# First MLP product computed token-major, with a seven-product two-by-two scheme for half of its K pairs

## Chip, core and metric

One core of a Trainium2 chip runs the whole program. The metric is the device time of one execution in microseconds (us); below, "stage" means a stretch of that execution. In the profile PE is TensorE's matrix multiplication, PEld its weight load (the loading of the stationary operand), DVE is VectorE, ACT is ScalarE, POOL is GpSimd, SP is SyncE (here it only issues DMAs).

## What is computed

One layer on 256 tokens of width 2048: a token mixer (two groups of recurrent heads, between an input and an output projection), then a squared-ReLU MLP with 8192 hidden units, each around a residual. The change concerns the first product of the MLP.

```python
h = h + hybrid_token_mixer(rms_norm(h, norm_mix_w), ...)
n = rms_norm(h, norm_ffn_w)
h = h + jnp.square(jax.nn.relu(n @ w_ff1)) @ w_ff2     # (256, 2048) @ (2048, 8192), then @ (8192, 2048)
out = rms_norm(h, norm_final_w)
```

All data are float32. The row factor of the second norm is positive and is taken out of the product: the kernel multiplies by the weight column `norm_ffn_w` before the first product and by the squared row factor `fs` after the second one.

## The kernel before, in words

**Products in three parts.** A float32 operand is split into a rounded part `hi` (type fp32r, what TensorE reads) and a remainder `lo`. A product is then hi·hi + hi·lo + lo·hi, all added up in one PSUM bank. `split` (L111) makes the parts of a weight tile: ACT casts to `hi` (L117), then DVE subtracts, `lo = w - hi` (L118). Both read SBUF; the subtraction has two SBUF inputs.

**Weights.** The weight matrices stream through three buffers `w` of 1 MB (L85, L99), filled by DMAs of SP's queue in program order. A buffer is filled again when its last `split` is done. `hi`/`lo` have three buffers of 1024 columns each (`spool`, L86).

**Stages.** (1) The input projection and the mixer, L166 to L627. (2) The output projection, L643 to L670, in two halves `nh` of 1024 output columns: 16 K steps with 12 products of 512 columns each into four banks; at the end of a half DVE adds the banks to the residual `h` (L660), ACT squares for the norm (L662), PE transposes the half's eight 128-column blocks to feature-major (L669) and `to_T` (L161) evicts each to `hT` as hi (ACT, L162) and lo (DVE, L163). (3) The first MLP product, L689 to L706, below. (4) The second, L721 to L742: for each of 64 hidden blocks, 24 products with a token-major stationary operand `gs` and 512 moving weight columns, into eight banks; the last three blocks are held back and interleaved with the final norm and the stores.

**The first MLP product** works feature-major: the weights stand still, the tokens move. Sixteen groups `fg` of four hidden blocks; a group reads four weight tiles; each K block and hidden block costs one matmul with `hi` stationary and 512 moving columns (the 256 tokens' hi and lo side by side, L700) and one with `lo` stationary and 256 moving columns (L701). At the end of a group ACT and DVE evict: copy, add, and `max(x,0)*x` into `g` (L703 to L706). So the hidden activations come out with the hidden unit on the partition, as the second product wants its stationary operand. POOL has no work in stages 3 and 4 except two tiny powers at the end.

**Order.** The Tile framework schedules the instructions of each engine from the data dependences and its own estimates, so the order of an engine's queue is not the text's; each engine runs its queue in order. PSUM has eight banks: four in `psA` and four in `psB`.

The residual `h` stays in SBUF from the output projection to the end of the program.

Of the kernel before, what the change touches and what calls it, by code (L numbers as in the profile page):

```python
# [73 lines left out]
def hybrid_block(ctx: ExitStack, tc: tile.TileContext, x, xt, w_in, w_ab, params, w_out, w_ff1, w_ff2,  # L74
# [555 lines left out]
    psB = ctx.enter_context(tc.tile_pool(name="psB", bufs=4, space=PSUM))  # L630
# [4 lines left out]
    hT = bpool.tile([P, KT, 2 * T], F32R, tag="xT", name="hT")
    h = bpool.tile([P, 2 * D], F32, tag="h", name="h").rearrange("p (f c) -> p f c", f=2)
    for hf in range(2):
        SP.dma_start(h[:, hf, :], x[hf * P:(hf + 1) * P, :])
    octx = ExitStack()
    op = octx.enter_context(tc.tile_pool(name="op", bufs=1))  # L640
    sqj = op.tile([P, 1024], F32, tag="sqj", name="sqj")
    fs = cpool.tile([P, 16], F32, tag="fs", name="fs")
    for nh in range(2):  # L643
        accs = [acc_a() for _ in range(4)]
        for kp in range(8):
            w = wtile()
            SP.dma_start(w, w_out[nh * 8 + kp])
            for kk in range(2):
                k = 2 * kp + kk
                hi, lo = split(w[:, kk * 1024:(kk + 1) * 1024], 1024)  # L650
                for hf in range(2):
                    for a, ww in ((0, hi), (T, hi), (0, lo)):
                        st = yT(k, a + hf * P, a + hf * P + P)
                        for c in range(2):
                            PE.matmul(accs[2 * hf + c], lhsT=st, rhs=ww[:, c * 512:(c + 1) * 512],  # L655
                                      start=(k == 0 and a == 0 and ww is hi), stop=(k == 2 * NH - 1 and ww is lo))
        for hf in range(2):
            for c in range(2):
                hv = h[:, hf, nh * 1024 + c * 512:nh * 1024 + (c + 1) * 512]
                DVE.tensor_tensor(out=hv, in0=accs[2 * hf + c], in1=hv, op=ALU.add)  # L660
            hv = h[:, hf, nh * 1024:(nh + 1) * 1024]
            ACT.activation(sqj, hv, AF.Square, accum_out=fs[:, 2 * hf + nh:2 * hf + nh + 1])  # L662
        for k2 in range(4):
            pt = acc_b()
            for kk in range(2):
                k = nh * 8 + k2 * 2 + kk
                ptk = pt[:, kk * T:(kk + 1) * T]
                for hf in range(2):
                    PE.transpose(ptk[:, hf * P:(hf + 1) * P], h[:, hf, k * P:(k + 1) * P], ident)  # L669
                to_T(hT, k, ptk, cols[:, 16 + k:17 + k])  # L670
# [7 lines left out]


    fp = ctx.enter_context(tc.tile_pool(name="fp", bufs=1))  # L680
    NF = DFF // P
    NG = NF // 2
    gt = [fp.tile([P, NG, T], F32, tag=f"g{i}", name=f"g{i}") for i in range(2)]

    def g(f):
        return gt[f // NG][:, f % NG, :]

    nfw = fp.tile([P, D], F32, tag="nfw", name="nfw")
    for fg in range(NF // 4):  # L689
        accs = [acc_a() if fg % 2 == 0 else acc_b() for _ in range(4)]  # L690
        for kq in range(4):
            w = wtile()
            SP.dma_start(w, w_ff1[fg * 4 + kq])
            for q in range(2):
                hi, lo = split(w[:, q * 1024:(q + 1) * 1024], 1024)
                for kk in range(2):
                    k = 4 * kq + 2 * q + kk
                    for f in range(4):
                        cs = slice(kk * 512 + f * P, kk * 512 + (f + 1) * P)
                        PE.matmul(accs[f], lhsT=hi[:, cs], rhs=hT[:, k, :], start=(k == 0), stop=False)  # L700
                        PE.matmul(accs[f][:, T:], lhsT=lo[:, cs], rhs=hT[:, k, 0:T], start=False, stop=(k == KT - 1))  # L701
        for f in range(4):
# [6 lines left out]
    accs = [[acc_a() for _ in range(4)], [acc_b() for _ in range(4)]]  # L709
    TAIL = 3  # L710
    held = []

# [5 lines left out]
                      start=(f == 0 and a == 0 and ww is hi), stop=(f == NF - 1 and ww is lo))  # L718

    keep = None  # L720
    for f in range(NF):  # L721
        w = wtile()
        SP.dma_start(w, w_ff2[f])
        gs = fp.tile([P, 2 * T], F32R, tag="gs", name="gs", bufs=4)
        split(g(f), None, gs[:, 0:T], gs[:, T:])
# [4 lines left out]
        for q in range(2):  # L730
            qs = slice(q * 1024, (q + 1) * 1024)
            if 0 <= n < TAIL - 1:
                hl.append(split(w[:, qs], None, keep[:, n, 0, qs], keep[:, n, 1, qs]))
            else:
                hl.append(split(w[:, qs], 1024))
        if n >= 0:
            held.append((f, gs, hl))
            continue
        for q in range(2):
            for hf in range(2):  # L740
                for c in (2 * q, 2 * q + 1):
                    ff2(f, hf, c, gs, hl)  # L742
    fin = fp.tile([P, 12], F32, tag="fin", name="fin")
    sqf = fp.tile([P, 512], F32, tag="sqf", name="sqf")
    o = fp.tile([P, D], F32, tag="o", name="o", bufs=1)
# [30 lines left out]
def _laid_out(i):  # L776
# [5 lines left out]
    for base in (0, 4112):  # L782
        v = w[:, base:base + 4096].reshape(2, 8, P, 2, 2, NH, P)
        groups.append(v.transpose(5, 3, 0, 2, 1, 4, 6).reshape(4 * NH, P, 2048))

    def columns(a):
        return a.reshape(-1, P).T

# [34 lines left out]
```

## Time and profile before

| | |
|---|---|
| median of 3 runs (lowest, highest) | 1283.92 us (1283.6, 1284.52) |
| the profiled execution | 1285.84 us |
| its span, first to last instruction | 1283.9 us |
| mean granted TensorE clock | 0.992 of full speed |
| stage 1, to the first output projection product | 455 us |
| stage 2 | 455 to 563.8 us |
| stage 3, the first MLP product | 563.8 to 926.8 us |
| stage 4, the second, and the end | 926.8 to 1283.9 us |

All durations below come from the profiled execution; its span is within 0.1 us of the runs' median, so a difference worked out on the span is applied to the median. Matmuls are pipelined: a 512-column matmul is shown with some 0.39 us, but the next one starts after a little over half of that, so what counts is the distance of starts. Times in brackets in a timeline row are idle time of the engine ahead of the instruction and what ended it.

### The profile page before, as it was taken

The page shows a single profiled execution, that of the slowest core. Times are in us where ns is not written, and L with a number is a line of the kernel's source. Part 1 is how long each engine was busy: PE and PEld are TensorE (multiplying, and loading weights), DVE is VectorE, ACT ScalarE, POOL GpSimd, SP SyncE. Part 2 cuts the span into 40 slices and gives each one's busy share as a digit, 9 for nine tenths or more (in the row PEclk, how much of TensorE's full clock was granted, in tenths as well). Part 3 has the DMA queues.
Part 4 walks back from the last instruction along what each step waited for, and adds up shares of the span by engine and source line. Part 5 has one row for each costly group of instructions (what it writes and reads, how often), then busy time and mean ns, then how long its engine had stood idle before and what let it go on. Part 6 is the DMA issues. An engine that isn't in the chain of part 4 may idle for free.

```text
span 1283.9 us, 18498 instructions
## 1 busy us (share of the span) xinstructions
PE 1252.5 (98%) x7290; PEld 1063.2 (83%) x7290; DVE 858.5 (67%) x1200; ACT 673.8 (52%) x972; POOL 180.4 (14%) x224
## 2 busy tenths in 40 slices
PE   6999999998899999999999999999999999999997
PEld 5888888877788887888888888888888888888885
DVE  8789999888867996565556555565555555555556
ACT  7567677655556874454444443444444444444453
POOL 4233433278301121000000000000000000000000
PEclk9999999998999999999999999999999999999999
DMA  7455555543423644455555555555555555555552
GB/s 289 166 160 184 174 180 192 171 140 131 149 100 131 217 151 168 154 203 191 194 173 190 196 174 189 197 175 186 197 195 190 188 191 192 194 194 197 197 200 95
DMA packets 34646, 229.65 MB, mean 179 GB/s; under 512 B 4408, under 2 KB 5184, under 8 KB 7808
## 3 DMA queue, kind: packets, MB, share of 16 engines
q1 hardware_dynamic: 32256, 225.32, 49.8%
q0 software_dynamic: 1728, 2.11, 1.3%
q8 instruction: 57, 0.93, 0.3%
q10 hardware_dynamic: 576, 1.05, 0.2%
q14 instruction: 29, 0.24, 0.1%
HBM read 225.83 MB, written 2.63 MB: 178 GB/s over the span
## 4 chain that ended last, share of the span: by engine, by line
PE 91%; DVE 3%; POOL 3%; issue 2%; DMA 1%; ACT 0%; SPq 0%; POOLq 0%; DVEq 0%; ACTq 0%
PE acc L281 15%; PE acc L717 14%; PE accb L717 13%; PE accb L700 9%; PE acc L700 9%; PE acc L282 8%; PE acc L655 7%; PE accb L701 5%; PE acc L701 5%; POOL Xt L419 1%; POOL X L421 1%; PE pd L575 1%; DVE xT L163 1%; DMA big<-in_xt_dram 1%; PE pk L363 1%
## 5 line engine op out<-in xcount | busy, mean ns | idle before, releaser
L118 DVE TENSOR_TENSOR lo<-w,hi 128x1024 fp32r<-128x1024 f32 x408 | 511.5, 1255 | 364.6 <-ACT hi L117 364.1
L117 ACT CAST hi<-w 128x1024 fp32r<-128x1024 f32 (+1 forms) x416 | 432.6, 1042 | 447.3 <-PE accb L717 177.2
L281 PE MATMUL acc<-xT,hi 128*128 128x512 f32 x1024 | 363.2, 401 | 9.6 <-ACT hi L117 8.5
L282 PE MATMUL acc<-xT,lo 128*128 128x256 f32 x1024 | 282.8, 285 | 4.8 <-DVE lo L118 4.7
L281 PEld LDWEIGHTS acc<-xT,hi 128*128 128x128 f32 x1024 | 191.0, 190 | 49.1 <-ACT hi L117 8.5
L282 PEld LDWEIGHTS acc<-xT,lo 128*128 128x128 f32 x1024 | 194.8, 191 | 12.1 <-DVE lo L118 6.2
L700 PE MATMUL acc<-hT,hi 128*128 128x512 f32 x512 | 181.3, 399 | 0.0
L700 PE MATMUL accb<-hT,hi 128*128 128x512 f32 x512 | 180.8, 398 | 0.0
L717 PE MATMUL accb<-hi,gs 128*128 128x512 f32 x496 | 170.6, 389 | 0.0
L701 PE MATMUL accb<-hT,lo 128*128 128x256 f32 x512 | 143.2, 281 | 0.0
L701 PE MATMUL acc<-hT,lo 128*128 128x256 f32 x512 | 142.8, 281 | 0.0
L717 PE MATMUL acc<-hi,gs 128*128 128x512 f32 x496 | 133.4, 389 | 0.0
L700 PEld LDWEIGHTS accb<-hT,hi 128*128 128x128 f32 x512 | 96.1, 188 | 23.9
L700 PEld LDWEIGHTS acc<-hT,hi 128*128 128x128 f32 x512 | 96.1, 188 | 23.4
L159 POOL TENSOR_TENSOR fin<-fin,cst 128x1 f32<-128x1 f32 x2 | 1.1, 566 | 777.0 <-PE accb L717 769.5
L717 PEld LDWEIGHTS acc<-hi,gs 128*128 128x128 f32 x496 | 93.0, 188 | 19.4
L717 PEld LDWEIGHTS accb<-hi,gs 128*128 128x128 f32 x496 | 93.1, 188 | 19.3
L701 PEld LDWEIGHTS acc<-hT,lo 128*128 128x128 f32 x512 | 96.5, 189 | 0.2
L701 PEld LDWEIGHTS accb<-hT,lo 128*128 128x128 f32 x512 | 96.6, 189 | 0.1
L717 PE MATMUL accb<-lo,gs 128*128 128x512 f32 x248 | 95.8, 389 | 0.0
L717 PE MATMUL acc<-lo,gs 128*128 128x512 f32 x248 | 77.2, 389 | 0.0
L717 PEld LDWEIGHTS acc<-lo,gs 128*128 128x128 f32 x248 | 46.6, 188 | 9.7
(248 smaller groups left out, 1323.6 us busy)
## 6 DMA issues: line engine op xcount, KB each, us to landing
w<-in_w_ff_dram SPq DMA_DIRECT2D x128, 1024.0 KB, 4.9
w<-in_w_in_dram SPq DMA_DIRECT2D x62, 1024.0 KB, 5.0
w<-in_w_out_dram SPq DMA_DIRECT2D x16, 1024.0 KB, 4.9
big<-in_xt_dram SPq DMA_DIRECT2D x4, 512.0 KB, 7.9
w<-in_w_in_dram SPq DMA_DIRECT2D x4, 512.0 KB, 8.1
h<-in_x_dram SPq DMA_DIRECT2D x2, 1024.0 KB, 9.2
dt<-scr_g POOLq DMA_DIRECT2D x8, 128.0 KB, 5.6
nfw<-in_norm_final_w_dram SPq DMA_DIRECT2D x1, 1024.0 KB, 4.7
```

Source lines behind the costliest of these rows:

```text
L117: ACT.copy(hi, w)
L118: eng.tensor_tensor(out=lo, in0=w, in1=hi.bitcast(F32), op=ALU.subtract)
L163: DVE.scalar_tensor_tensor(out=dst[:, k, T:2 * T], in0=pt, scalar=wcol, in1=dst[:, k, 0:T].bitcast(F32), op0=ALU.mult, op1=ALU.subtract)
L281: PE.matmul(accs[g], lhsT=hi[:, kk, g, :], rhs=xT[:, k, :], start=(k == 0), stop=False)
L282: PE.matmul(accs[g][:, T:], lhsT=lo[:, kk, g, :], rhs=xT[:, k, 0:T], start=False, stop=(k == KT - 1))
L363: PE.matmul(pk0, lhsT=R[:, 1, 0:P], rhs=qk.rearrange("p a t -> p (a t)"), start=True, stop=True)
L419: POOL.tensor_tensor(out=t3, in0=X[:, j, j + 1:].unsqueeze(2).to_broadcast([np_, nr, ncol]), in1=X[:, j, 0:ncol].unsqueeze(1).to_broadcast ...
L421: POOL.tensor_tensor(out=X[:, j + 1:, 0:ncol], in0=X[:, j + 1:, 0:ncol], in1=t3, op=ALU.subtract)
L655: PE.matmul(accs[2 * hf + c], lhsT=st, rhs=ww[:, c * 512:(c + 1) * 512], start=(k == 0 and a == 0 and ww is hi), stop=(k == 2 * NH - 1 and ...
L700: PE.matmul(accs[f], lhsT=hi[:, cs], rhs=hT[:, k, :], start=(k == 0), stop=False)
L701: PE.matmul(accs[f][:, T:], lhsT=lo[:, cs], rhs=hT[:, k, 0:T], start=False, stop=(k == KT - 1))
L717: PE.matmul(accs[hf][c], lhsT=gs[:, a + hf * P:a + hf * P + P], rhs=ww[:, cs], start=(f == 0 and a == 0 and ww is hi), stop=(f == NF - 1 a ...
```

## The change

The first MLP product is turned round. The tokens (128 at a time) become the stationary operand and 512 weight columns move; the result is token-major, so PE has to transpose it afterwards. The 2048-long contraction is taken in eight pairs `kp` of two 128-blocks, one weight tile each, and the hidden units in eight groups `ng` of 1024, that is two blocks of 512. For a pair, the activations are a 2×2 block matrix (two token halves × two K blocks) and the weights another (two K blocks × two hidden blocks).

- Four pairs (2, 4, 6, 7) are multiplied plainly: 8 block products of three matmuls, 24 matmuls of 512 columns.
- Four pairs (`SUMS`: 0, 1, 3, 5) use a Winograd-Strassen scheme with seven block products, 21 matmuls. It needs sums of the activation blocks (made once, at the end of the output projection, and kept as `sets`) and four sums of the weight blocks for each tile. The weight sums T1, T2, T4 and one in place are made by POOL, each a 128x512 tensor_tensor with two SBUF inputs; they and the original blocks are split as before, 3.5 times 1024 columns for a tile instead of 2.
- Each of the seven products has a bank of its own; after the last of the four pairs DVE combines p1, p5, p6, p7 in `C4`, and after the last pair it adds p2, p3, p4, p8. ACT applies relu. The transposes (16 for a group, in four bundles, with ACT's square as eviction) are put between products of the next group as `fills`, through bank 8.
- `h` no longer stays in SBUF: each half goes to DRAM (`scr_h`) as soon as it is summed, and comes back, with the last norm's weights, after the last product that reads `sets`, by loads on SP's queue.
- The hi/lo pairs have two more buffers (five); the constants come in two DMAs, the larger part in a buffer that is given up after stage 1. All eight PSUM banks are one pool in stages 3 and 4.

```diff
+            X = op.tile([P, 8, P], F32, tag="X", name="X", bufs=2)
+            ACT.activation(view(X, P, [[-P, 2], [1, P]]), pt[:, 0:T].rearrange("p (a t) -> p a t", a=2), AF.Copy, scale=wc[0])
+            ACT.activation(X[:, 2:4, :].rearrange("p a t -> p (a t)"), pt[:, T:2 * T], AF.Copy, scale=wc[1])
+            DVE.tensor_tensor(out=X[:, 4], in0=X[:, 0], in1=X[:, 3], op=ALU.add)
...
+            split(X[:, 1:8], None, st[:, 0], st[:, 1])
...
+        pool, t = (spool, "") if n % 5 < 3 else (fp, "2")
+        return [pool.tile([P, 1024], F32R, tag=p + t, name=p + t, bufs=2 if t else 3) for p in ("hi", "lo")]
...
+    def product(dst, a, b, start, stop):
+        (ah, al), (bh, bl) = a, b
+        PE.matmul(dst, lhsT=ah, rhs=bh, start=start, stop=False)
+        PE.matmul(dst, lhsT=al, rhs=bh, start=False, stop=False)
+        PE.matmul(dst, lhsT=ah, rhs=bl, start=False, stop=stop)
...
+            for c in range(4):
+                PE.transpose(pt[:, c * P:(c + 1) * P], src[:, c * P:(c + 1) * P], ident)
+            ACT.activation(g(8 * ng + 4 * half, 4)[:, :, hf * P:(hf + 1) * P], pt.rearrange("p (c t) -> p c t", c=4),
+                           AF.Square)
...
-                        PE.matmul(accs[f], lhsT=hi[:, cs], rhs=hT[:, k, :], start=(k == 0), stop=False)
-                        PE.matmul(accs[f][:, T:], lhsT=lo[:, cs], rhs=hT[:, k, 0:T], start=False, stop=(k == KT - 1))
-        for f in range(4):
-            lot = fp.tile([P, T], F32, tag="lotf", name="lotf", bufs=2)
-            ACT.copy(lot, accs[f][:, T:])
-            DVE.tensor_tensor(out=lot, in0=accs[f][:, 0:T], in1=lot, op=ALU.add)
-            DVE.scalar_tensor_tensor(out=g(4 * fg + f), in0=lot, scalar=0.0, in1=lot, op0=ALU.max, op1=ALU.mult)
+            SP.dma_start(w, w_ff1[ng * KP + kp])
...
+                POOL.tensor_tensor(out=T1, in0=b12, in1=w[:, 512:1024], op=ALU.subtract)
+                POOL.tensor_tensor(out=T2, in0=b22, in1=T1, op=ALU.subtract)
+                POOL.tensor_tensor(out=T4, in0=b21, in1=T2, op=ALU.subtract)
+                POOL.tensor_tensor(out=b12, in0=b22, in1=b12, op=ALU.subtract)
+                B21, B22 = halves(split_pair(w[:, 1024:2048]))
+                B1, B2 = halves(split_pair(TT[:, 0:1024]))
+                B4 = [tp.tile([P, 512], F32R, tag=t, name=t) for t in ("hi4", "lo4")]
+                split(T4, None, *B4)
+                B3, B11 = halves(split_pair(w[:, 0:1024]))
...
+                for dst, a, b in ((p2, 1, B21), (p3, 6, B22), (p5, 3, B1), (p6, 4, B2), (p4, 2, B4), (p7, 5, B3),
+                                  (p1, 0, B11)):
+                    product(dst, A[a], b, kp == 0, kp == LAST_SUMS and a in (0, 3, 4, 5))
...
+                for kk, b1, b2 in ((0, B11, B12), (1, B21, B22)):
+                    for dst, hf, b in ((p2, 0, b1), (p3, 0, b2), (p4, 1, b1), (p8, 1, b2)):
+                        product(dst, A(kk, hf), b, first and kk == 0 and dst is p8, last and kk == 1)
+        for n, (at, p) in enumerate(((0, p2), (2, p3), (1, p4), (3, p8))):
+            DVE.tensor_tensor(out=C4[:, at], in0=p, in1=C4[:, at], op=ALU.add)
+        for n in range(4):
+            ACT.activation(C4[:, n], C4[:, n], AF.Relu)
+            fills.append(turn(ng, n, C4[:, n]))
+    for hf in range(2):
+        SP.dma_start(h[:, hf, :], scr_h[hf])
```

The order of instructions moves most at three places.

PE at the seam between stages 2 and 3. Before (L655: output projection; L669: transposes of the second half; L700, L701: first MLP product):

```order
L655 MATMUL acc<-hi,yTb 128x512 x4
L655 MATMUL acc<-lo,yTb 128x512 x2
L669 MATMUL accb<-cst,h 128x128 x2
L700 MATMUL acc<-hT,hi 128x512
L701 MATMUL acc<-hT,lo 128x256
```

Now (L675, L690 and L756 to L758 in their places):

```order
L675 MATMUL acc<-hi,yTb 128x512 x4
L675 MATMUL acc<-lo,yTb 128x512 x2
L690 MATMUL accb<-cst,h 128x128 x16
L756 MATMUL p_5701<-hi,sets 128x512
L757 MATMUL p_5701<-hi,sets 128x512
L758 MATMUL p_5701<-lo,sets 128x512
```

The sixteen transposes stood in eight pairs between products of the next stage; now they stand in one row, and the first MLP product is behind all of them.

DVE in the middle of the first MLP product. Before, one group (L705, L706: the eviction):

```order
L118 TENSOR_TENSOR lo<-w,hi 128x1024 x7
L705 TENSOR_TENSOR lotf<-accb,lotf 128x256 x2
L706 SCALAR_TENSOR_TENSOR g_5652<-lotf 128x256 x2
L118 TENSOR_TENSOR lo<-w,hi 128x1024
```

Now, from the end of one group to the third tile of the next (L120 is `split`'s subtraction; `TT` holds the weight sums T1, T2, T4; `C` is C4, `p` a bank):

```order
L829 TENSOR_TENSOR C_7026<-p_6751,C_7026 128x512
L829 TENSOR_TENSOR C_7026<-p_6752,C_7026 128x512
L120 TENSOR_TENSOR lo_7135<-w,hi_7134 128x1024
L829 TENSOR_TENSOR C_7026<-p_6753,C_7026 128x512
L120 TENSOR_TENSOR lo_7179<-w,hi_7178 128x1024
L829 TENSOR_TENSOR C_7026<-p_6879,C_7026 128x512
L120 TENSOR_TENSOR lo_7131<-TT,hi_7130 128x512
L120 TENSOR_TENSOR lo<-TT,hi 128x1024
L120 TENSOR_TENSOR lo_7234<-w,hi_7233 128x1024
L120 TENSOR_TENSOR lo<-w,hi 128x1024 x2
L120 TENSOR_TENSOR lo_7187<-TT,hi_7186 128x512
L120 TENSOR_TENSOR lo_7270<-w,hi_7269 128x1024
```

The splits of a group are no longer alone: the bank additions stand among them, and splits of `TT`, which POOL must have written.

POOL before: the last rows of stage 1 (L550, L599), then the two powers of the final norm (L159):

```order
L538 TENSOR_TENSOR u<-u 128x256
L541 TENSOR_SCALAR gx<-gx 128x256
L550 TENSOR_TENSOR E<-gx 128x256
L599 TENSOR_TENSOR A<-rd,cst 128x128 x2
L159 TENSOR_TENSOR fin<-fin,cst 128x1 x2
```

Now, after stage 1 (L703: activation sums of the output projection; L788 to L791: the weight sums of tile 0; L791 is the one in place):

```order
L603 TENSOR_TENSOR A<-rd,cst_a 128x128 x2
L703 TENSOR_TENSOR X<-X 128x128 x3
L788 TENSOR_TENSOR TT<-w 128x512
L789 TENSOR_TENSOR TT<-w,TT 128x512
L791 TENSOR_TENSOR w<-w 128x512
L790 TENSOR_TENSOR TT<-w,TT 128x512
```

The last four stand there thirty-two times, sixteen rows for each of the eight groups, where POOL had nothing.

More of the change, by code (lines that the diff above doesn't have):

```diff
@@ L627, in hybrid_block, with a_plain, a_sums @@
     mctx.close()
[L630 removed]
+    octx = ExitStack()
+    psB = octx.enter_context(tc.tile_pool(name="psB", bufs=4, space=PSUM))
     def acc_b():
         return psB.tile([P, 512], F32, tag="accb", name="accb")
[L635 to L636 removed]
+    SUMS = (0, 1, 3, 5)
+    sets = bpool.tile([P, 8192], F32R, tag="xT", name="sets")
+    sets2 = ctx.enter_context(tc.tile_pool(name="ap", bufs=1, side="right")).tile([P, 3584], F32R, tag="s2", name="sets2")
+    plain = [kp for kp in range(KT // 2) if kp not in SUMS]
+    def a_plain(kp):
+        n = plain.index(kp)
+        return sets[:, n * 1024:(n + 1) * 1024].rearrange("p (k s) -> p k s", k=2)
+    def a_sums(kp):
+        n = SUMS.index(kp)
+        t, at = (sets, 4096 + n * 1792) if n < 2 else (sets2, (n - 2) * 1792)
+        return t[:, at:at + 1792].rearrange("p (s n t) -> p s n t", s=2, n=7)
+    h = hpool.tile([P, 2 * D], F32, tag="h", name="h").rearrange("p (f c) -> p f c", f=2)
+    scr_h = dpool.tile([2, P, D], F32, tag="scr_h", name="scr_h")
     for hf in range(2):
         SP.dma_start(h[:, hf, :], x[hf * P:(hf + 1) * P, :])
[L639 removed]
     op = octx.enter_context(tc.tile_pool(name="op", bufs=1))
@@ new lines, in g, with bank, pair, split_pair @@
+    def g(f, n=1):
+        return gt[f // NG][:, f % NG:f % NG + n, :]
+    def bank(i):
+        return psF.tile([P, 512], F32, tag=f"p{i}", name=f"p{i}")
+    pairs = [0]
+    def pair():
+        n = pairs[0] = pairs[0] + 1
+        pool, t = (spool, "") if n % 5 < 3 else (fp, "2")
+        return [pool.tile([P, 1024], F32R, tag=p + t, name=p + t, bufs=2 if t else 3) for p in ("hi", "lo")]
+    def split_pair(w):
+        hi, lo = pair()
+        split(w, None, hi, lo)
+        return hi, lo
@@ new lines, in halves, with turn, go @@
+    def halves(hl):
+        return [[t[:, c * 512:(c + 1) * 512] for t in hl] for c in range(2)]
+    def turn(ng, n, src):
+        half, hf = n // 2, n % 2
+        def go():
+            pt = bank(8)
+            for c in range(4):
+                PE.transpose(pt[:, c * P:(c + 1) * P], src[:, c * P:(c + 1) * P], ident)
+            ACT.activation(g(8 * ng + 4 * half, 4)[:, :, hf * P:(hf + 1) * P], pt.rearrange("p (c t) -> p c t", c=4),
+                           AF.Square)
+        return go
@@ L707, in hybrid_block @@
+    t1.close()
+    f2 = ctx.enter_context(tc.tile_pool(name="f2", bufs=1, side="right"))
+    tail = bpool.tile([P, 8192], F32, tag="xT", name="tail")
+    h, nfw, o = tail[:, 0:2 * D].rearrange("p (f c) -> p f c", f=2), tail[:, 2 * D:3 * D], tail[:, 3 * D:]
+    for hf in range(2):
+        SP.dma_start(h[:, hf, :], scr_h[hf])
     SP.dma_start(nfw, norm_final_w.unsqueeze(0).to_broadcast([P, D]))
-    accs = [[acc_a() for _ in range(4)], [acc_b() for _ in range(4)]]
+    accs = [[None] * 4, [None] * 4]
@@ L710, in hybrid_block @@
+    for hf, c, i in ((0, 0, 1), (0, 1, 5), (1, 0, 6), (1, 1, 7), (0, 2, 2), (0, 3, 3), (1, 2, 4)):
+        accs[hf][c] = bank(i)
     TAIL = 3
@@ L720, in hybrid_block @@
     keep = None
+    late = []
     for f in range(NF):
@@ L734, in hybrid_block @@
             else:
-                hl.append(split(w[:, qs], 1024))
+                hl.append(split_pair(w[:, qs]))
         if n >= 0:
@@ L741, in hybrid_block @@
                 for c in (2 * q, 2 * q + 1):
[L742 to L745, printed above, removed]
+                    if f < 2 and (hf, c) == (1, 3):
+                        late.append((f, hf, c, gs, hl))
+                    else:
+                        ff2(f, hf, c, gs, hl)
+                    fill()
+        if f == 1:
+            accs[1][3] = bank(8)
+            for a in late:
+                ff2(*a)
+            c1.close()
+    fin = f2.tile([P, 12], F32, tag="fin", name="fin")
+    sqf = f2.tile([P, 512], F32, tag="sqf", name="sqf")
     NP = 5
```

91 lines of the change are left out of this document (69 added, 22 removed).

## The prediction

> **What bounds the kernel now.** I read the page first: busy times, and the share of the chain that ended last.
>
> ```profile
> span 1283.9 us, 18498 instructions
> PE 1252.5 (98%) x7290; PEld 1063.2 (83%) x7290; DVE 858.5 (67%) x1200; ACT 673.8 (52%) x972; POOL 180.4 (14%) x224
> PE 91%; DVE 3%; POOL 3%; issue 2%; DMA 1%; ACT 0%; SPq 0%; POOLq 0%; DVEq 0%; ACTq 0%
> ```
>
> PE ends the program. Busy matmuls overlap, so the stages tell more: the windows of stage 3 and of stage 4's products, then the same windows for L118 (DVE's remainder subtraction) alone.
>
> ```profile
> core 0: us, PE busy (x) PEld busy (x) DVE busy (x) ACT busy (x) POOL busy (x), PEclk, DMA share, GB/s
> 563.80:926.80 363.00, 363.00 (x2065) 315.00 (x2064) 205.22 (x270) 160.30 (x206) 0.00 (x0) 1.00 0.54 189
> 926.80:1274.90 348.10, 348.10 (x1538) 288.07 (x1536) 187.67 (x212) 156.85 (x203) 0.58 (x1) 1.00 0.54 188
> 563.80:926.80 363.00, 158.24 (x132) 0.00 (x0) 1.00 0.54 189
> ```
>
> In stage 3 PE never idles at a full clock (1.00), DVE works 205 of 363 us, POOL nothing. The waits say who is late:
>
> ```profile
> ACT hi L117 <- PE accb L700: 95.2, 64, 1.8
> ACT hi L117 <- PE acc L700: 92.0, 62, 1.8
> ```
>
> ACT waits for PE to free a buffer, never PE for a split: stage 3 is bound by PE alone, with 158 us of DVE idle and a free POOL. What the change is worth is fewer PE cycles, as long as DVE and POOL keep up.
>
> **The change part by part.**
>
> *PE, removed and added.* Stage 4 has the form that stage 3 takes now: activations stationary, 512 weight columns moving. Its 1536 products take 348.1 us, so 0.2266 us each. Stage 3 now has, for each of eight groups, 4 × 21 + 4 × 24 = 180 such products, 1440 in all: 326.3 us. [...]
>
> The new transposes are priced by the old ones in stage 3:
>
> ```profile
> 564.81 0.28 PE L701 MATMUL acc<-hT,lo 128*128 128x256 f32 x1
> 565.17 0.28 PE L701 MATMUL acc<-hT,lo 128*128 128x256 f32 x1
> 565.29 0.38 PE L669 MATMUL accb<-cst,h 128*128 128x128 f32 x2
> 565.75 0.28 PE L701 MATMUL acc<-hT,lo 128*128 128x256 f32 x1
> ```
>
> From L701 to L701 it is 0.36 us without and 0.58 us with two transposes between: 0.11 us each. The change has 128 (16 a group): 14.1 us. PE's work is 340.4 us against 363.0: 22.6 us less, 42.55 us a group. With no new waits that would be the gain.
>
> *The seam.* All eight banks are handed from stage 2 to stage 3, and the first product now stands behind all sixteen transposes and, through the banks, behind their evictions. The rows that price it:
>
> ```profile
> 563.15 0.61 PE L655 MATMUL acc<-lo,yTb 128*128 128x512 f32 x2
> 563.79 0.48 PE L700 MATMUL acc<-hT,hi 128*128 128x512 f32 x1
> L660 DVE TENSOR_TENSOR h<-acc,h 128x512 f32<-128x512 f32 x8 | 5.1, 684 | 3.4 <-PE acc L655 3.4
> L662 ACT ACTIVATE sqj<-h 128x1024 f32<-128x1024 f32 x4 | 4.2, 1058 | 0.1
> 565.26 0.18 ACT L662 ACTIVATION_READ_ACCUMULATOR sqj<-h 128x1 f32 x1
> L162 ACT ACTIVATE hT<-accb,prm 128x256 fp32r<-128x256 f32 x16 | 6.6, 471 | 5.0 <-PE accb L669 5.0
> L163 DVE SCALAR_TENSOR_TENSOR hT<-accb,prm,hT 128x256 fp32r<-128x256 f32 x16 | 6.9, 478 | 5.4 <-ACT hT L162 5.4
> ```
>
> Before, stage 3's first product starts 0.64 us after the last ones of stage 2. Now ACT has, one after the other: a cast in progress (0.6), two squares (2.1, and 0.18 each to read their sums), eight evictions of 0.47 (3.8); then DVE's last remainder, 0.48: 7.3 us. As PE gets 0.64 us of that already, 6.7 us are new, and the sixteen old transposes (1.8 us) lie inside. Nothing covers this.
>
> *DVE and POOL, added.* A group has 4 × 3.5 + 4 × 2 = 22 splits of 1024 columns (20 whole, 4 halves) where the same share of work had 16, and eight bank additions like L660; POOL has 16 sums of 128x512. Alone, each engine has room. But see what a POOL operation and a split do to each other in stage 1 (L339 is a POOL subtraction 128x512 with two SBUF inputs; L289 is DVE with one input in PSUM):
>
> ```profile
> L118 DVE TENSOR_TENSOR lo<-w,hi x408: 1198/1225/2336, 25.5 to 1257.4; 128x1024 fp32r<-128x1024 f32 x136
> 108.94 2.34 DVE L118 TENSOR_TENSOR lo<-w,hi 128x1024 fp32r<-128x1024 f32 x1 [0.27 <-ACT hi L117]
> 108.90 1.29 POOL L339 TENSOR_TENSOR slo<-u,shi 128x512 fp32r<-128x512 f32 x1
> 131.45 1.76 DVE L118 TENSOR_TENSOR lo<-w,hi 128x1024 fp32r<-128x1024 f32 x1
> 133.14 0.41 DVE L289 TENSOR_TENSOR lot<-acc,lot 128x256 f32<-128x256 f32 x1
> 133.47 1.97 DVE L118 TENSOR_TENSOR lo<-w,hi 128x1024 fp32r<-128x1024 f32 x1
> 132.10 2.26 POOL L339 TENSOR_TENSOR slo<-u,shi 128x512 fp32r<-128x512 f32 x1
> 134.32 1.72 POOL L290 TENSOR_TENSOR pre<-lot,rB 128x256 f32<-128x256 f32 x1
> ```
>
> At 108.9 POOL starts first and takes 1.29 us; the split, started 0.04 us later, takes 2.34 instead of 1.22. At 132.1 the split is first: POOL ends at 134.36, 1.15 us after the split's end at 133.21; the next split, issued at 133.47, ends at 135.44, 1.08 us after POOL. L289 at 133.14 is not held up. So a POOL sum and a split exclude each other, taking turns, 1.15 and 1.08 us; a bank addition runs beside POOL. For each group that is one row of work: 20 × 1.08 + 4 × 0.6 + 16 × 1.15 = 42.4 us, as long as PE's 42.55. Nothing is left over, and neither side can run far ahead: five hi/lo pairs, three weight buffers.
>
> How much is lost I worked through a group in the orders of the queues, with three more prices:
>
> ```profile
> L117 ACT CAST hi<-w 128x1024 fp32r<-128x1024 f32 x408 | 428.2, 1051 | 447.3 <-PE accb L717 177.2 <-PE accb L700 95.2 <-PE acc L700 92.0
> w<-in_w_ff_dram SPq DMA_DIRECT2D x128, 1024.0 KB, 4.9
> h<-in_x_dram SPq DMA_DIRECT2D x2, 1024.0 KB, 9.2
> ```
>
> The load of tile 0 is issued when DVE has split tile 5's last pair of the group before; call that 0. It lands at 4.9; POOL's T1 runs to 6.2, a split to 7.3, T2 to 8.45, ACT's cast to 9.5. PE, busy with tiles 6 and 7, reaches tile 0's first T product at 12.4, so this is in time. But from 7.3 on sums and splits alternate without a gap: ten sums and seven and a half splits, to the first remainder of tile 2, 10 × 1.15 + 7 × 1.08 + 0.6 = 19.7 us, so to some 27.2. PE needs the remainder of tile 1's last pair at 22.6 and gets it at 24.95 (wait 2.35), and that of tile 2 at 25.85, getting it at 27.2 (1.35). Tile 5's four sums delay tile 4's split by another 0.8. The sum of waits is 4.5 us a group, and the group ends with DVE as far ahead as it began. Begun with DVE 3.3 us later, the same chain gives 9.1 us of waits. I take 4.5, since the chain settles there; 9.1 is the upper end, 0 the lower.
>
> *At nothing.* The loads of `h` and the norm weights (3 MB) stand on SP ahead of the second product's fifth tile: 9.2 + 4.9 + 4.9 = 19 us against four tiles of PE, 4 × 24 × 0.2266 = 21.8; without that cover 2 to 4 us, once. The stores of `h` wait on SP for DVE's additions; three loaded tiles cover what is behind. Those stores must land before the two new buffers can be written; 24 products (5.4 us) after the seam cover most. The second constants load changes no queue but SP's, at the start. ACT gains work but has 200 us free. Stage 4 has the same products.
>
> *The sum.* Stage 3: 8 × (42.55 + 4.5) + 6.7 = 383.1 us, against 363.0: +20.1. The profiled execution took 1285.84 us with a span of 1283.9, the runs' median is 1283.92; the difference goes on the median: 1304.
>
> **The rivals.**
>
> *POOL is hidden (faster).* If POOL's sums, which write f32 and not fp32r, do not hold up the splits, DVE has 20 × 1.22 + 12 × 0.68 = 32.6 us of work a group and PE sets the pace: −22.6 + 6.7 = −15.9, 1268. It decides if a split beside a sum takes about 1.2 us. For it: the L339 rows write fp32r. Against: L290 writes f32 and takes 1.72 us for half the columns when a split is beside it. [...] Milder forms end here too: waits below 1.5 us a group, if queue orders happen to fit.
>
> *The chain does not settle (slower still).* DVE comes late to each group, waits for the last bank and then finds POOL ahead: 9.1 us of waits a group, 8 × 51.65 + 6.7 = 419.9, +56.9: 1341. For it: the additions of a group's end wait for PE's last product, with the next group's splits behind them. Against: DVE has four such splits done by then.
>
> *The queues don't do what the text says*, and PE has more matmuls than I count: the built order shows 1440 products and 128 transposes, so I give it nothing.
>
> **How the numbers follow.** A measurement can tell about 0.2%, 2.6 us. Forecast with waits of 3 to 8 us a group: 0.55, slower. Hidden POOL and its milder forms: 0.27, faster. Waits of 1.6 to 2.3 us a group, within 0.2%: 0.05. The unsettled chain: 0.13, slower. Faster 0.27, same 0.05, slower 0.68. The range goes from the hidden POOL's 1268 to 1335, which is waits of 8.4 us a group; the forecast's own is 1292 to 1332. The prediction is 1304.
>
> **What would show it.** Right: in stage 3 splits beside POOL sums of over 2 us and POOL sums over 2 us where a split was first; bank additions at 0.68; PE idle some 4 to 5 us a group on remainders (L758 on `lo`, mostly tiles 1 and 2), a wait of about 7 us at the seam, and a stage of about 383 us. Wrong: POOL sums of 1.3 us beside splits of 1.22, PE without waits, a stage below 350 us. The prediction falls if PE waits for loads, if a product's distance isn't 0.227 us, or if the waits are of another engine.

## The result and the profile after

The changed kernel takes 1320.49 us (median of 4 runs, 1318.48 to 1321.46) against 1283.76 beside it: 1.0285 times as long, 95% interval 1.0268 to 1.0303. The forecast was 1304, slower, with a range to 1335. The profiled execution took 1320.52 us, with a span of 1318.5 us; all differences below are between its span and the 1283.9 us of before. One execution of the run `two_first` below came at a granted clock of 0.844 and took 1404.72 us; the median given there is that of the other three.

The page's head, engine times and the chain that ended last:

```profile
span 1318.5 us, 17871 instructions
PE 1253.2 (95%) x6810; PEld 1035.2 (79%) x6810; DVE 990.8 (75%) x1208; ACT 738.9 (56%) x1048; POOL 430.4 (33%) x356
PE 70%; POOL 10%; DVE 8%; issue 5%; DMA 4%; ACT 2%; SPq 0%; POOLq 0%; DVEq 0%; ACTq 0%
```

PE's busy time is that of before (1252.5), although it has 480 matmuls fewer, and its share of the chain fell from 91% to 70%: POOL stands on the path now with 10% and DVE with 8%, where each had 3%. The windows say where (the seam, stage 3, the products of stage 4; columns as in the prediction), and the last row has the splits (L120) of stage 3 alone:

```profile
563.30:573.30 10.00, 4.19 (x18) 2.93 (x17) 9.22 (x19) 7.18 (x14) 3.57 (x3) 0.82 0.26 105
573.30:958.50 385.20, 356.56 (x1552) 282.07 (x1553) 325.60 (x259) 215.00 (x262) 233.35 (x120) 0.99 0.50 175
958.50:1309.80 351.30, 350.34 (x1554) 289.74 (x1552) 185.68 (x208) 157.69 (x206) 0.58 (x1) 1.00 0.56 194
573.30:958.50 385.20, 290.39 (x196) 0.00 (x0) 0.99 0.50 175
```

Between the last product of the output projection and the first of the MLP lie 10.0 us where there were 0.4: +9.6. Stage 3 takes 385.3 us from its first product to the first of stage 4, where it took 363.0: +22.3. The second product takes 351.0 from its first to its last start where it took 347.9: +3.1. The end is 0.3 shorter. These parts make 34.7 us; the spans differ by 34.6.

Four rows of the waits of stage 3 (who waited for whom: us, times, longest) name both POOL and DVE:

```profile
ACT hi L119 <- POOL TT L789: 50.1, 24, 3.7
PEld p L758 <- DVE lo L120: 25.5, 18, 3.1
PE p L758 <- DVE lo L120: 17.9, 16, 2.6
PE p L756 <- ACT hi L119: 8.1, 8, 1.7
```

PE waits for remainders and, less, for casts; the casts wait for POOL's sums. Before, ACT waited for PE and PE for nobody. To count the stops, take the distance from the start of each of the 1440 products to the start of PE's next instruction, product or transpose. What these distances have beyond 0.227 us, over all above 0.26, is 42.3 us in stage 3: 5.3 us a group. By group it is 1.5, 9.0, 5.9, 5.5, 4.7, 5.3, 4.9 and 5.4. The count leaves out 2.2 us of stops that come right behind a transpose, and it holds 3.8 us of products that are slow after a stop (last section).

How the sums and the splits stand to each other, in the settled fifth group (the timeline of POOL, then of DVE):

```profile
763.88 2.29 POOL L790 TENSOR_TENSOR TT<-w,TT 128x512 f32<-128x512 f32 x1
772.37 2.27 POOL L790 TENSOR_TENSOR TT<-w,TT 128x512 f32<-128x512 f32 x1
774.60 2.28 POOL L788 TENSOR_TENSOR TT<-w 128x512 f32<-128x512 f32 x1
763.78 1.23 DVE L120 TENSOR_TENSOR lo<-TT,hi 128x1024 fp32r<-128x1024 f32 x1 [2.27 <-ACT hi L119]
764.92 1.28 DVE L829 TENSOR_TENSOR C<-p,C 128x512 f32<-128x512 f32 x2
771.83 1.66 DVE L120 TENSOR_TENSOR lo<-TT,hi 128x1024 fp32r<-128x1024 f32 x1 [0.56 <-ACT hi L119]
773.42 6.78 DVE L120 TENSOR_TENSOR lo<-w,hi 128x1024 fp32r<-128x1024 f32 x3
```

The split of 763.78 ends at 765.01, the sum behind it at 766.17, 1.16 us later; two bank additions meanwhile take 1.28 us together, 0.60 from start to start, as they do alone. From 773.42 on three splits alternate with sums and take 2.26 us each. This is the picture that the prediction drew from stage 1.

### The profile page after: what moved, and what is told of

It reads as the page before. It is cut to its first block, busy times and chain, and to the rows that moved or that the text cites. A ratio compares the mean times of both kernels' runs of the same rounds, so it can differ in the third digit from the quotient of the medians.

```text
span 1318.5 us, 17871 instructions
## 1 busy us (share of the span) xinstructions
PE 1253.2 (95%) x6810; PEld 1035.2 (79%) x6810; DVE 990.8 (75%) x1208; ACT 738.9 (56%) x1048; POOL 430.4 (33%) x356
## 4 chain that ended last, share of the span: by engine, by line
PE 70%; POOL 10%; DVE 8%; issue 5%; DMA 4%; ACT 2%; SPq 0%; POOLq 0%; DVEq 0%; ACTq 0%
PE p L851 26%; PE acc L285 16%; PE acc L286 8%; PE acc L675 5%; DVE lo L120 5%; DMA w<-in_w_ff_dram 4%; PE p L758 3%; PE p L756 3%; PE p L757 3%; POOL TT L789 3%; POOL TT L788 2%; POOL TT L790 2%; POOL w L791 1%; ACT hi L119 1%; PE pd L579 1%
## 5 line engine op out<-in xcount | busy, mean ns | idle before, releaser
L120 DVE TENSOR_TENSOR lo<-w,hi 128x1024 fp32r<-128x1024 f32 x408 | 564.5, 1396 | 229.4 <-ACT hi L119 224.8
L851 PE MATMUL p<-hi,gs 128*128 128x512 f32 x992 | 304.7, 389 | 1.0 <-ACT g L771 1.0
L851 PEld LDWEIGHTS p<-hi,gs 128*128 128x128 f32 x992 | 186.0, 188 | 39.6 <-ACT g L771 1.2
L756 PE MATMUL p<-hi,sets 128*128 128x512 f32 x480 | 191.3, 401 | 11.9 <-ACT hi L119 8.1
L851 PE MATMUL p<-lo,gs 128*128 128x512 f32 x496 | 191.9, 389 | 0.0
L757 PE MATMUL p<-hi,sets 128*128 128x512 f32 x480 | 189.8, 396 | 0.0
L758 PE MATMUL p<-lo,sets 128*128 128x512 f32 x480 | 168.4, 402 | 18.1 <-DVE lo L120 17.9
L758 PEld LDWEIGHTS p<-lo,sets 128*128 128x128 f32 x480 | 89.5, 190 | 43.2 <-DVE lo L120 25.5
L756 PEld LDWEIGHTS p<-hi,sets 128*128 128x128 f32 x480 | 91.3, 190 | 38.3 <-ACT hi L119 14.0
L120 DVE TENSOR_TENSOR lo<-TT,hi 128x1024 fp32r<-128x1024 f32 (+1 forms) x64 | 84.9, 1337 | 33.2 <-ACT hi L119 33.1
L788 POOL TENSOR_TENSOR TT<-w 128x512 f32<-128x512 f32 x32 | 58.9, 1840 | 152.2 <-DMA w<-in_w_ff_dram 133.0
L851 PEld LDWEIGHTS p<-lo,gs 128*128 128x128 f32 x496 | 93.0, 188 | 19.4
L757 PEld LDWEIGHTS p<-hi,sets 128*128 128x128 f32 x480 | 91.3, 190 | 19.2
L790 POOL TENSOR_TENSOR TT<-w,TT 128x512 f32<-128x512 f32 x32 | 67.8, 2120 | 0.0
L789 POOL TENSOR_TENSOR TT<-w,TT 128x512 f32<-128x512 f32 x32 | 63.7, 1992 | 2.5
```

Source lines behind the costliest of these rows:

```text
L120: eng.tensor_tensor(out=lo, in0=w, in1=hi.bitcast(F32), op=ALU.subtract)
L756: PE.matmul(dst, lhsT=ah, rhs=bh, start=start, stop=False)
L757: PE.matmul(dst, lhsT=al, rhs=bh, start=False, stop=False)
L758: PE.matmul(dst, lhsT=ah, rhs=bl, start=False, stop=stop)
L788: POOL.tensor_tensor(out=T1, in0=b12, in1=w[:, 512:1024], op=ALU.subtract)
L789: POOL.tensor_tensor(out=T2, in0=b22, in1=T1, op=ALU.subtract)
```

## Experiments

Theory A is the prediction's: sums and splits take turns, and in stage 3 their common row of work is as long as PE's. Against it stand theory B (three weight buffers and five pairs are too short a lead, whatever POOL does) and theory C (what costs is the length of the chain load, T1, T2, cast, subtraction). "Seam" below is the distance from the last output projection product to the first MLP product, "waits" are counted as above. `no_sums`, `idle_sums`, `memset` and `mixed` are one execution each. Where the seam begins, the profiled executions already differ by up to 3.8 us (560.2 to 564.0), so stage 3 says more than a single total.

### Without the sums

```diff
-                POOL.tensor_tensor(out=T1, in0=b12, in1=w[:, 512:1024], op=ALU.subtract)
...
-                B1, B2 = halves(split_pair(TT[:, 0:1024]))
+                B1, B2 = halves(split_pair(w[:, 0:1024]))
...
-                split(T4, None, *B4)
+                split(w[:, 1024:1536], None, *B4)
```

> The 128 weight sums are left out: the same 28 splits of a group read the blocks of the weight tile itself, products, transposes, evictions and seam stay (the result is not the layer's). Theory A, turns between POOL's sums and DVE's splits: stage 3's 42 us of waits of PE go to under 6 us, splits take 1.22 us throughout, and the seam loses the 2.3 us by which DVE's additions came late; 1318.5 - 36 to 39 - 2 = about 1279 us, 1274 to 1284. Theory B, three weight buffers and five pairs are too short a lead for 28 splits and eight additions whatever POOL does: waits of 3 us a group or more stay, 1300 us or more.

Measured: 1275.8 us, span 1273.8. The windows of its stage 3, all engines and then L120 alone:

```profile
568.79:913.50 344.71, 344.71 (x1552) 283.21 (x1553) 249.21 (x259) 215.16 (x261) 0.00 (x0) 0.99 0.56 198
568.79:913.50 344.71, 213.12 (x197) 0.00 (x0) 0.99 0.56 198
```

The same splits take 213 us instead of 290, and PE hardly stops: the waits are 4.9 us. Without waits the stage is 339.8 us, against 340.4 of PE work in the forecast. Theory B falls. The seam is 7.2 us.

### Sums that nobody reads

```diff
-                POOL.tensor_tensor(out=b12, in0=b22, in1=b12, op=ALU.subtract)
+                POOL.tensor_tensor(out=T1, in0=b22, in1=b12, op=ALU.subtract)
```

and the splits read `w`, as in the run before.

> POOL makes all 128 sums from the same blocks and at the same places, but nobody reads them: the splits read the weight tile itself (the result is not the layer's). So the turns of the two engines stay and the chain load, T1, T2, cast, subtraction is gone. Theory A, the turns: total stays near the changed kernel's, 1306 to 1322 us, with splits beside a sum at over 2 us. Theory C, the chain's length (a split of TT can't start before two or three sums are done): total falls to that of the kernel without sums, 1274 to 1286 us, though splits beside sums stay long.

Measured: 1305.03 us, 1 us under theory A's band and 19 over theory C's. Stage 3, all engines and L120:

```profile
568.54:943.20 374.66, 350.19 (x1552) 280.92 (x1553) 340.29 (x258) 213.81 (x261) 232.37 (x120) 1.00 0.51 181
568.54:943.20 374.66, 304.38 (x196) 0.00 (x0) 1.00 0.51 181
```

Of the 44.7 us between the run without sums and the changed kernel, 29.2 are there when nothing depends on the sums; by seam and stage 3 alone it is 31.1 of 43.3. The waits are 34.4 us, 4.8 in each of the last six groups. Theory C is not the main cause. But it has a part: with the chain, waits are 42.3 us, 5 of the 8 us more in the second group (9.0 against 4.0). There 2.3 us are a wait of transposes for an eviction of ACT, which stood behind a cast that had waited 4.0 us for POOL's sum.

### The sums on DVE

```diff
-                POOL.tensor_tensor(out=T1, in0=b12, in1=w[:, 512:1024], op=ALU.subtract)
+                DVE.tensor_tensor(out=T1, in0=b12, in1=w[:, 512:1024], op=ALU.subtract)
```

and the other three likewise.

> The same sums, made by DVE instead of POOL: the data chain stays, the two engines no longer share anything. DVE's row of work for a group, by its back-to-back distances (a split 1.15 us, a half one, an addition or a sum 0.60 each): 20 x 1.15 + 28 x 0.60 = 39.8 us against PE's 42.6. Theory A, the turns: waits fall from 5.3 to 1.5 us a group or less, 1281 to 1293 us, so near the kernel before. Theory C, the chain: waits stay at 4 us a group or more, 1308 us or more. In between, 1295 to 1305: DVE's row is too close to PE's to run ahead.

Measured: 1276.74 us, better than expected and faster than the kernel before: ratio 0.9942, 0.9926 to 0.9959. Its stage 3, and DVE's row in it:

```profile
568.90:914.04 345.14, 344.92 (x1552) 283.06 (x1553) 316.23 (x380) 217.31 (x263) 0.00 (x0) 0.99 0.56 198
710.60 0.69 DVE L789 TENSOR_TENSOR TT<-w,TT 128x512 f32<-128x512 f32 x1
711.20 0.70 DVE L791 TENSOR_TENSOR w<-w 128x512 f32<-128x512 f32 x1
711.80 0.70 DVE L790 TENSOR_TENSOR TT<-w,TT 128x512 f32<-128x512 f32 x1
714.55 2.36 DVE L120 TENSOR_TENSOR lo<-w,hi 128x1024 fp32r<-128x1024 f32 x2
```

A sum takes 0.60 us from start to start on DVE, where on POOL it holds the splits for 1.15. DVE does all the work that two engines did, in 316 us instead of 326, and waits fall to 5.2 us, 0.4 a group once it is settled. The chain is whole here, so its length costs next to nothing by itself; it costs beside the turns.

### POOL writes, but reads nothing

```diff
-                POOL.tensor_tensor(out=T1, in0=b12, in1=w[:, 512:1024], op=ALU.subtract)
+                POOL.memset(T1, 0.01)
```

and the others likewise, the one in place first.

> POOL writes constants where it wrote the sums: the splits still wait for POOL's instruction, but POOL reads nothing from SBUF and the sums no longer hang on one another or, but for the one in place, on the load (the result is not the layer's). If POOL's reads make the turns: splits stay at 1.22 us beside them, 1274 to 1284 us. If any POOL instruction takes turns with DVE's splits, writing ones too: splits over 2 us beside them, 1295 us or more.

Measured: 1276.3 us. The groups of the splits in stage 3 (ns, least, median, most), and of one of POOL's instructions:

```profile
L120 DVE TENSOR_TENSOR lo<-w,hi x127: 1216/1224/1228, 572.9 to 909.0; 128x1024 fp32r<-128x1024 f32 x127
L789 POOL MEMSET TT<- x32: 518/527/532, 513.2 to 880.4; 128x512 f32 x32
```

No split is lengthened, and the memsets lie within 14 ns of each other. A pair side by side:

```profile
709.39 0.53 POOL L791 MEMSET TT<- 128x512 f32 x1
709.52 1.22 DVE L120 TENSOR_TENSOR lo<-w,hi 128x1024 fp32r<-128x1024 f32 x1
```

Beside memsets a split took 1.22 us, beside sums that read SBUF 2.26 in the changed kernel. So in these two runs it was not a busy POOL that held DVE up but one that reads, as far as one memset of 0.53 us can stand for a sum that takes 1.29 while DVE is idle (612.28 in the changed kernel).

### Half of the sums on POOL, in two ways

First by pairs, with the scheme for two pairs only:

```diff
-    SUMS = (0, 1, 3, 5)
+    SUMS = (0, 3)
```

> The seven-product scheme for two of the eight pairs (0 and 3) instead of four, POOL making the 64 sums that are left; the result is the layer's. PE's work is 8 x 6 x 0.227 = 10.9 us more than with four. The row of turns loses two times 4 x 1.15 + 1.5 x 1.08 = 12.4 us a group: 30.0 us against PE's 43.9. Theory A, turns cost only where their row fills PE's time: waits under 8 us in all, total 1318.5 - 42 + 11 + 5 = about 1292, 1284 to 1296 us. If each sum costs PE the same, half the waits stay: 21 us, 1302 to 1310 us.

Measured: 1301.86 us (ratio 1.0139, 1.0121 to 1.0156), at the edge of the other reading's band. But of its 13.7 us of waits only 1.0 stand before L758, that is on remainders, where the changed kernel has 23.1. What it waits for instead stands in the waits of stage 3:

```profile
PE p L770 <- ACT g L771: 5.5, 8, 1.4
PE p L756 <- ACT g L771: 3.7, 5, 0.8
```

With pair 1 multiplied plainly, all four bundles of transposes come ahead of it through one bank, and PE waits for their evictions: a cost of my choice of pairs. So I took the first two pairs, once with POOL's sums and once with DVE's:

```diff
-    SUMS = (0, 1, 3, 5)
+    SUMS = (0, 1)
```

> The scheme for pairs 0 and 1 only, POOL's sums, the result is the layer's. The run with pairs 0 and 3 kept 13.7 us of waits, but only 1.0 us of them on remainders; 5 were on the transposes of the group before, which that order drew together at pair 1. Here they have two tiles' time again, as in the changed kernel. Theory A (turns cost only where their row fills PE's time): 1318.5 - 42 + 11 + 3 to 6, so 1290 to 1294 us, remainder waits under 3 us. If the transposes are not what was left, 1298 to 1304 as before.

Measured: 1298.3 us, ratio 1.0101 (1.0082 to 1.0119), above what I expected.

> The scheme for pairs 0 and 1 with the sums made by DVE, the result is the layer's. The same with POOL's sums took 1298.3 us (median of the undisturbed runs), 4 to 8 us over what was expected. If POOL's turns still cost there, though they fill only 30 of PE's 43.9 us: dve_sums has 345.1 us in stage 3 and a seam of 7.3, 48 more products are 10.9 us, so 1276.7 + 10.9 = about 1287 us, 1284 to 1290. If it is the order of products, transposes and evictions with fewer pairs: 1295 us or more.

Measured: 1294.67 us (ratio 1.0081, 1.0063 to 1.0099). My sum missed by 8 us again, now without POOL: its seam is 9.6 instead of 7.3 us, and the transposes with the steps to and from them take 23.2 us of stage 3 where `dve_sums` has 17.1. That is the order of the work, as the rival said: at its seam two casts and two splits of weights stand between the evictions. What counts for theory A is the difference of the two runs: with half the sums, POOL's turns cost some 3.6 us, with intervals that overlap; with all of them, 1320.5 against 1276.7, they cost 43.8. Turns cost much here where their row fills PE's time, and little where it fills two thirds.

Then by kind, T1 and T2 on POOL, the other two on DVE:

```diff
-                POOL.tensor_tensor(out=T4, in0=b21, in1=T2, op=ALU.subtract)
-                POOL.tensor_tensor(out=b12, in0=b22, in1=b12, op=ALU.subtract)
+                DVE.tensor_tensor(out=T4, in0=b21, in1=T2, op=ALU.subtract)
+                DVE.tensor_tensor(out=b12, in0=b22, in1=b12, op=ALU.subtract)
```

> Four pairs again; POOL makes T1 and T2, DVE T4 and the sum in place, the result is the layer's. Row of turns for a group: 20 x 1.08 + 4 x 0.6 + 8 x 1.15 + 8 x 0.60 = 38.0 us against PE's 42.6, where the changed kernel has 42.4. Theory A: waits of PE go from 42 us to 5 to 15, total 1281 to 1292 us. If each POOL sum costs its share (half of 37 us on top of 5), 24 us of waits, about 1300.

Measured: 1323.61 us. Both numbers are missed: the waits are 42.3 us by the same count as in the changed kernel, 26.4 of them now before L756, which waits for casts, and 7.1 us more stand behind transposes, where the changed kernel has 2.2. The rows of one group, POOL, DVE, ACT and PE:

```profile
770.86 4.32 POOL L788 TENSOR_TENSOR TT<-w 128x512 f32<-128x512 f32 x1 [7.78 <-DMA w<-in_w_ff_dram]
770.55 1.21 DVE L120 TENSOR_TENSOR lo<-TT,hi 128x1024 fp32r<-128x1024 f32 x1
771.68 2.35 DVE L120 TENSOR_TENSOR lo<-w,hi 128x1024 fp32r<-128x1024 f32 x2
775.21 0.69 DVE L791 TENSOR_TENSOR w<-w 128x512 f32<-128x512 f32 x1 [1.18 <-POOL TT L788]
777.05 0.69 DVE L790 TENSOR_TENSOR TT<-w,TT 128x512 f32<-128x512 f32 x1 [1.15 <-POOL TT L789]
777.05 1.04 ACT L119 CAST hi<-TT 128x1024 fp32r<-128x1024 f32 x1 [4.15 <-POOL TT L789]
778.15 0.50 PE L756 MATMUL p<-hi,sets 128*128 128x512 f32 x1 [3.48 <-ACT hi L119]
```

T1 comes behind three splits in a row and is done 1.1 us after the last of them. DVE's sum in place overwrites what T1 reads, so DVE itself waits, with its splits queued behind; the cast of T1 and T2 comes late, and PE stands idle for 3.5 us before 778.15. The sum of a row says how much work there is, not that the queues can do it without waiting for each other: that is where my use of theory A failed, since I counted this run only by the row.

### Token-major alone

```diff
-    SUMS = (0, 1, 3, 5)
+    SUMS = ()
...
-                        product(dst, A(kk, hf), b, first and kk == 0 and dst is p8, last and kk == 1)
+                        product(dst, A(kk, hf), b, first and kk == 0, last and kk == 1)
+                        if kk or kp:
+                            fill()
...
+            ACT.activation(C4[:, at], p, AF.Relu)
```

with banks that alternate by group.

> The turn to token-major alone: all eight pairs by 24 products, no sums, no seven-product scheme, ACT evicts with relu; the result is the layer's. 1536 x 0.2266 + 14.1 = 362.2 us of PE work, as long as the 363.0 before; a seam of some 7 us and 3 to 5 us of waits are on top: 1290 to 1297 us. All of the gain would then be the scheme's 96 x 0.2266 = 21.8 us. If token-major has a cost or gain of its own in PE's pace, the stage is over 372 or under 358 us.

Measured: 1292.59 us, ratio 1.0066 (1.0049 to 1.0083). Stage 3 by the windows:

```profile
570.94:933.82 362.88, 362.88 (x1648) 300.43 (x1649) 158.71 (x133) 167.12 (x192) 0.00 (x0) 1.00 0.54 186
```

362.9 us against 363.0 before: turning the product round neither gains nor loses in stage 3. What makes the kernel slower is the seam (7.0 us where it was 0.4) and the second product, which takes 2.6 us longer. All that the change can gain comes from the seven products, 17.7 us of stage 3 from here to `dve_sums`, where the expectation had 21.8.

### The seam

The banks come from the two pools of four that stage 2 uses, instead of one new pool of eight that waits for all of them; the squares stand behind the evictions.

```diff
-    psF = ctx.enter_context(tc.tile_pool(name="psF", bufs=1, space=PSUM))
...
-        return psF.tile([P, 512], F32, tag=f"p{i}", name=f"p{i}")
+        return acc_a() if i in (2, 3, 5, 6) else acc_b()
```

> The changed kernel with its banks taken from the two pools of four that stage 2 uses, instead of one new pool of eight, and with ACT's squares behind the evictions in the text: the first products need only the banks of the output projection, not the last eviction of the transposes. If the seam's 9.5 us are its own cost, some 5 to 8 us go: 1312 to 1316 us. If PE then only runs earlier into the splits that POOL's sums hold up, it is given back in the first group: 1318 to 1321 us.

Measured: 1316.0 us, ratio 1.0242 (1.0221 to 1.0263): 4.5 us less than the changed kernel. Its profiled execution was the fastest of four (1311.7): the seam goes from 10.0 to 2.8 us and stage 3 is 2.7 us shorter, although PE, earlier now, waits 8.1 us in the first group where it waited 1.5; most later groups wait less. The second product takes 2.4 us more. The median stands at the upper edge of the first reading's band (1312 to 1316). The second reading is right about the first group only: in the profiled execution stage 3 as a whole gives nothing back. Why the other three executions are 3.7 to 5.7 us longer isn't shown, since only this one has a trace.

> DVE's sums and the seam's edit together, the result is the layer's. DVE's sums alone took 1276.7 us with a seam of 7.3 us; the seam's edit alone brought its kernel's to 2.8 us. If the two add up, 1272 us, 1270 to 1274, some 0.9% below the kernel before. If PE, started earlier, runs into splits that DVE hasn't done, or the rotating banks hold up the last group's transposes (the seam's kernel had 2.4 us more in the second product), 1275 to 1278.

Measured: 1272.77 us, ratio 0.9905 (0.9891 to 0.992). The two add up (4.0 us less than `dve_sums`). PE at its seam (L689: transposes, L757 to L759: products):

```profile
563.28 0.44 PE L689 MATMUL accb<-cst,h 128*128 128x128 f32 x2
563.47 0.48 PE L757 MATMUL acc<-hi,sets 128*128 128x512 f32 x1
...
571.33 0.50 PE L757 MATMUL accb<-hi,sets 128*128 128x512 f32 x1 [1.23 <-ACT hi L119]
572.73 0.50 PE L759 MATMUL accb<-lo,sets 128*128 128x512 f32 x1 [0.67 <-DVE lo L120]
575.20 0.50 PE L757 MATMUL accb<-hi,sets 128*128 128x512 f32 x1 [1.27 <-ACT hi L119]
```

The first product starts 0.5 us after the last one of stage 2, among the transposes, as before the change; three waits follow some 8 to 12 us later. The last run takes the four squares out of the seam:

```diff
-            ACT.activation(sqj, h[:, hf, nh * 1024:(nh + 1) * 1024], AF.Square,
-                           accum_out=fs[:, 2 * hf + nh:2 * hf + nh + 1])
...
+                ACT.activation(o, h[:, hf, :], AF.Square, accum_out=fs[:, 4 + hf:5 + hf])
```

the added line in the second product, at its thirteenth block.

> DVE's sums and the seam's edit, and the norm's four squares moved from the seam into the second product, made from the residual that is loaded there again; the result is the layer's. In the run with both edits PE still waits 3.7 us in the first group (1.4, 0.8 and 1.4) for casts and remainders, and ACT has 2.5 us of squares ahead of them. If they are why: 1269 to 1271.5 us. If the evictions alone fill ACT and DVE there: 1272 to 1274.

Measured: 1271.17 us, ratio 0.9898 (0.9881 to 0.9915), the fastest here, 13.7 us under the kernel before beside it. The three waits are 0.86, 0.67 and 0.88 us of idle time now. The step from the run before is 1.6 us, with intervals that overlap.

## Why the prediction was right, and which terms were off

**PE's work was right.** 340.4 us forecast; 339.8 measured in `no_sums`, where no sum holds PE up. Sixteen of the 128 transposes lie in the second product, though, and I had all of them in stage 3 and the second product "the same". By the forecast's prices stage 3 would then have 338.6 us, and the second product takes 3.1 us more, with a wait of 1.0 us for an eviction behind its last transposes. In the seam's price, the distance of 0.64 us before the change is 0.41 from the last start to the first.

**The mechanism was right.** Turns of POOL's sums and DVE's splits, read from the rows of stage 1, make PE wait: with POOL writing only, 42.3 us of waits become 5.0, and with the sums on DVE and their chain whole, 5.2. These runs take 1276 us, near the 1268 of the rival of a hidden POOL, but its premise is wrong: sums written in f32 do hold up splits (2.26 us). What frees PE is taking POOL's reading sums away. The mechanism is not the whole: `idle_sums` has turns without the chain and 34.4 us of waits, and the rest came with the chain.

**The waits were sized a little low.** 4.5 us a group were taken for every group (the hand-worked chain of 7.3 and 19.7 ends at 27.0 and not 27.2, which would make it 4.3). From the fourth on, groups have 4.7 to 5.5; in all it is 42.3 against 36.0. Of the 6.3 between them 3.8 are no waits but the slow products after stops, for which the prediction had no term. That the size comes so near has some luck in it, because the chain names waits for remainders at tiles 1, 2 and 4 and none for casts. The second group has 9.0, like the 9.1 of the chain that begins with DVE late; the likeness is in part chance, since 2.3 of it is the wait for an eviction. In the count, waits fall on casts too (12.8 us before L756), where the prediction had named remainders alone (23.1 before L758).

**The seam was sized low, by the same mechanism.** 6.7 us forecast, 9.6 measured. The chain of ACT and DVE was right: with the same pairs and without POOL's sums (`no_sums`, `memset`, `dve_sums`) the seam is 7.2 to 7.3 us, 6.9 more than before. What the sum left out is tile 1's sums in front of it:

```profile
560.74 2.32 DVE L120 TENSOR_TENSOR lo<-w,hi 128x1024 fp32r<-128x1024 f32 x1
562.98 2.30 DVE L120 TENSOR_TENSOR lo<-TT,hi 128x1024 fp32r<-128x1024 f32 x1
565.21 2.47 DVE L680 TENSOR_TENSOR h<-acc,h 128x512 f32<-128x512 f32 x4
561.94 2.26 POOL L791 TENSOR_TENSOR w<-w 128x512 f32<-128x512 f32 x1
564.17 2.25 POOL L790 TENSOR_TENSOR TT<-w,TT 128x512 f32<-128x512 f32 x1
```

Two splits of 2.3 us stand in DVE's queue ahead of the additions that the transposes wait for; undelayed they would have taken 2.2 us less together.

**At nothing, and rightly so:** the reload of `h`, its stores and the second load of the constants appear in no wait of PE, and the last product of stage 2 starts at 563.3 us where it started at 563.4.

The terms that were low add up to 14.6 us: 2.9 at the seam, 6.3 of waits, 2.6 in the rest of stage 3, of which 2.2 are the stops behind transposes, and 2.8 in the second product and the end. They make the 20.1 of the forecast the 34.7 that were measured.

## What to carry to other kernels

POOL's free time was no free resource here, because its sums and DVE's splits took turns, 1.15 and 1.08 us: add up the row of work that two engines share, with the time that each really holds the other, before moving work over; here the "busy" DVE did a sum in 0.60 us, about half the time for which POOL held it. A row as long as the critical engine's time cost some 5 us a group here, and one at two thirds little (3.6 us in all); but `mixed`, at nine tenths by its row, cost as much as the full one, because its queues waited for each other. And of the 22.6 us that PE's shorter work promised, 9.6 were spent where stage 2 hands over its banks: look there for what the first instruction of the new stage really waits for.

## What the runs showed of the hardware

**After the longest stops of PE the next products were slow.** PE after its wait of 681.69 in the changed kernel:

```profile
681.69 0.73 PE L758 MATMUL p<-lo,sets 128*128 128x512 f32 x2 [2.61 <-DVE lo L120]
682.26 0.59 PE L756 MATMUL p<-hi,sets 128*128 128x512 f32 x1
682.64 0.63 PE L757 MATMUL p<-hi,sets 128*128 128x512 f32 x1
683.07 0.63 PE L758 MATMUL p<-lo,sets 128*128 128x512 f32 x1
683.50 0.63 PE L756 MATMUL p<-hi,sets 128*128 128x512 f32 x1
683.92 0.63 PE L757 MATMUL p<-hi,sets 128*128 128x512 f32 x1
682.60:685.60 3.00, 3.00 (x8) 2.30 (x7) 3.00 (x3) 1.10 (x2) 2.40 (x2) 0.50 0.95 339
685.70:688.70 3.00, 3.00 (x17) 2.48 (x16) 3.00 (x3) 2.06 (x3) 2.06 (x1) 1.00 0.04 14
```

The distance of starts is 0.43 us instead of 0.227, for some 3 us, and the windows (the last two rows) show a granted clock of 0.50 in that time and 1.00 behind it. This came after each of the longest stops: 3.0 us from start to start here and at 730.34, 3.8 at the seam, 4.6 at the seam of `dve_sums`; not after 2.5 at 646.04. In stage 1 of the changed kernel it also came after a stop of 1.7 at 327.24, but not after one of 1.9 at 621.13 in stage 3, so the length of one stop is not all that counts. The windows behind these two stops, then the one behind 646.04:

```profile
327.40:330.60 3.20, 3.20 (x11) 2.82 (x12) 3.17 (x8) 2.11 (x3) 1.17 (x3) 0.50 0.93 264
621.20:624.40 3.20, 3.20 (x14) 2.54 (x15) 3.20 (x5) 2.53 (x4) 0.00 (x0) 1.00 0.66 212
646.10:649.30 3.20, 3.20 (x17) 2.70 (x18) 1.34 (x2) 1.33 (x2) 0.00 (x0) 1.00 0.54 225
```

Nineteen products of the changed kernel's stage 3 are so spaced, at 0.2 us each 3.8 us that a count of idle time does not hold, while the count of distances above does. What sets the granted clock was not shown.

**Turns are not always turns.** In the changed kernel sums and splits alternate: from 674.93 four splits take 8.94 us, 2.24 each. In `mixed` a sum stood behind a whole run of splits: T1 at 770.86 behind three, for 4.32 us, and the longest T1 took 5.24. Why they alternate in the one and not in the other was not shown.
